# Four feature tiles at once, a normalised pair per quarter step, an earlier second attention and eight first products

## The chip, the cores and the metric

The kernel runs on one core of one Trainium2 chip. The metric is the device time of one launch in microseconds (us); the kernel before is given as the median of 3 runs.

## The reference

Two chained networks of two layers each work on x of 256 tokens by 1024 features, in fp32. Cut to what matters here:

```python
# first block, each of 2 layers
u = rms_norm(h, norm_mix[layer])
z, xbc, dt_raw, q, k, v, g_ssd, g_attn = split(u @ w_in[layer])
y_ssd = ssd_mixer(z, xbc, dt_raw, ...)          # convolution, state space, gated norm
y_attn = dilated_attention_mixer(q, k, v, ...)  # 8 kv heads, 3 windows each
merged = sigmoid(g_ssd) * (y_ssd @ w_ssd_branch) + sigmoid(g_attn) * (y_attn @ w_attn_branch)
h = h + merged @ w_out[layer]
u = rms_norm(h, norm_ffn[layer])
gate, up = split(u @ w_gate_up[layer])
h = h + (silu(gate) * up) @ w_down[layer]
# second block, each of 2 layers
proj = rms_norm_2(x, norm_g[i]) @ w_in[i]       # retention heads and block-sparse attention heads
x = x + concat(r_out, m_out) @ w_out[i]
gate = sigmoid(rms_norm_2(x) @ w_ple_gate[i])
e = rms_norm_2(p[i] @ w_ple[i], ple_norm_g[i])
x = x + gate * e
```

## The kernel before

**Products.** All activations lie with features on the 128 partitions. Every fp32 product is three: weight and activation are each split into a rounded high part and a low remainder, and high·high, high·low and low·high are summed in PSUM. TensorE (PE) is the engine that nearly all of this runs on. The weights come in one stream, planned ahead: the DMA queue of SP brings 1 MB pieces (`raw`, 3 buffers), each holding two units of 1024 columns; for each unit ScalarE (ACT) casts the high part (`wh`, L154) and VectorE (DVE) subtracts it (`wl`, L157). Where `pool_every` is 4, in the state-space part of the first block, GpSimd (POOL) subtracts every fourth unit. Each of `wh` and `wl` has 3 buffers, and a split is called two units ahead (`LEAD`).

**Shapes of products.** `outT` (L411) makes eight output tiles of 128 features in the order of `blocks` (L47): for the three matrices of 1024 by 1024 that end in the residual or in the gate (`w_out`, `w_out_2`, `w_ple_gate_2`), three feature tiles run together over all eight input tiles (72 matmuls), then the other five one after the other. Each of the first four tiles has a PSUM buffer of its own in pool `mm`, which has 3 buffers; they are handed to `evac` by twos, when both are complete. Later tiles share a buffer by twos. `pairA` makes two feature tiles (L449 to L451); `slab` makes two token tiles of 512 columns, four units long (L394 to L396). PSUM has two more pools, `tr` (2 buffers, transposes) and `ch` (3, small products).

**Background steps.** Generators lie in queues `bg`; the products call `tick`, which moves each queue on by one `yield`. `Norm.part` squares finished feature pairs and writes `uh`, `ul`. `Norm.steps` sums over features with products of ones (L232), takes the power on POOL (`rsqrt`, L363, L369), spreads the factor over partitions (L223), and then either copies it (`rb`, L256: the gate of the second block) or, where `vpair` holds, makes all eight normalised tiles (`nv`, L262) and their splits (`uh` L376 on ACT, `ul` L387 on DVE). `norm_ple` (L1018) does the like for `e`, with the product L1042 behind the power `gr`.

**Places that the change touches.** At the start, products of ones (L324) run while the first weights come. In `block1` (L703) the heads of attention A run behind the projections of the second half; attention B begins at the last pair of the B projections (f == 6), after A's steps have been run out, with one `yield` more per head (`late`). Behind `w_out`, two slabs of `w_gate_up` (p = 0, 1) run on the unnormalised tiles, each followed by a tanh on ACT (L825) and two DVE products (L826, L827) that read its PSUM buffers. In `block2` (L1052) the gate's `evac` (L1102) first runs the norm's steps out and then, tile by tile, does L1110 (DVE, reads PSUM), tanh (L1111), L1112 and L1113.

**Order.** Only SP's issues at the start are in a written order; elsewhere a scheduler places instructions by its own reckoning of times, so that a change of the program's order or of a wait can move instructions far from it.

Of the kernel before, what the change touches and what calls it, by code (L numbers as in the profile page):

```python
# [10 lines left out]
F32 = mybir.dt.float32  # L11
# [3 lines left out]
ALU = mybir.AluOpType  # L15
# [3 lines left out]
P = 128  # L19
# [16 lines left out]
LEAD = 2  # L36
WARM = 2
START1 = 2
# [8 lines left out]
def blocks(name):  # L47

    kt = {"w_ple_2": 2, "w_down": 22}.get(name)
    if kt:  # L50
        return [(k, f) for f in range(8) for k in range(kt)]
    pairs = (4, 6, 0, 2) if name == "w_out_2" else (0, 2, 4, 6)
    out = [(k + i, f) for k in pairs for f in range(3) for i in range(2)]
    return out + [(k + i, f) for f in range(3, 8) for k in pairs for i in range(2)]

# [116 lines left out]
class Norm:  # L172
# [73 lines left out]
    def steps(self, wait=1):  # L246
        net, nc = self.net, self.net.nc
        for _ in range(wait):
            yield
        self.factor()  # L250
        for _ in range(wait):
            yield
        rb = self.broadcast(self.r)
        if not self.vpair:
            self.rb = net.sp.tile([P, S], F32, tag="cb", name="rb")
            nc.scalar.copy(self.rb, rb)  # L256
            return
        self.vh, self.vl = net.pair([P, KD, S], "uh", "ul")
        for f in range(0, 8, 2):
            v = net.sp.tile([P, 2, S], F32, tag="qk", name="nv", bufs=QK_BUFS)  # L260
            for i in range(2):
                nc.vector.scalar_tensor_tensor(v[:, i, :], self.h[:, f + i, :], self.gain[:, f + i:f + i + 1], rb,  # L262
                                               ALU.mult, ALU.mult)
            net.split(self.vh[:, f:f + 2, :], self.vl[:, f:f + 2, :], v)
        if self.first:
            for _ in range(8):
                yield
            rb = self.broadcast(self.r1)
            for f in range(8):
                h = self.h[:, f, :]  # L270
                nc.vector.scalar_tensor_tensor(h, h, self.first[0][:, f:f + 1], rb, ALU.mult, ALU.mult)
                if f % 2:
                    yield
# [7 lines left out]
class Net:  # L281
# [129 lines left out]
    def outT(self, name, layer, get, evac, ticks=1):  # L411
# [7 lines left out]
        for n, (k, f) in enumerate(seq):  # L419
# [3 lines left out]
            if b not in bank:  # L423
                bank[b] = self.mm.tile([P, 2, S], F32, tag="mm", name="mm")
            ps = bank[b][:, f - b, :]
# [6 lines left out]
            if (n + 1) % (8 // ticks) == 0:  # L432
                self.tick()
            f &= ~1
            if left[f] == 0 and left[f + 1] == 0:
                if f < single:
                    evac(f, [(i, 1, bank.pop(i)[:, 0:1, :]) for i in (f, f + 1)])
                else:
                    evac(f, [(f, 2, bank.pop(f))])

# [54 lines left out]

    def attention(self, v, kT, q0, q1, q2, oh, ol, late=0):
        nc = self.nc
# [3 lines left out]
        for h in range(4):  # L501
# [26 lines left out]
            yield  # L528
            for _ in range(late):
                yield  # L530
            pt = self.transpose4([e[:, 0, 256:384], e[:, 0, 0:128], e[:, 0, 128:256]])
# [171 lines left out]
    def block1(self, l, h, n1):  # L703
# [32 lines left out]
        for f in range(0, 8, 2):  # L736
            ps = self.pairA("w_in", l, C_B + 128 * f, D, getu)
            self.conv_pair(l, ps, 16 + f, bc[:, f:f + 2, :])
            if f == 6:
                self.drain(qa)  # L740
                os.append(self.pair([P, 4, S], "A0", "A1"))
                qa.append(self.attention(*B, *os[1], 1))
        def halves(tiles):
# [110 lines left out]
    def add_half(self, h, norm):  # L854
        def evac(f, parts):
            for i, n, ps in parts:
                hf = h[:, i:i + n, :]
                self.nc.vector.scalar_tensor_tensor(hf, ps, 0.5, hf, ALU.mult, ALU.add)
            norm.part(f)
        return evac  # L860
# [144 lines left out]
    def ple(self, l):  # L1005

        ph, pl = self.pair([P, 2, S], f"A{2 * l}", f"A{2 * l + 1}")
        self.split(ph, pl, self.pT[l])
        e = [self.sp.tile([P, 4, S], F32, tag=f"B{2 * l + t}", name="e") for t in range(2)]
        self.e0.append(e)  # L1010

        def evac(f, parts):
            ps = parts[0][2]
            (self.nc.scalar.copy if f % 4 else self.nc.vector.tensor_copy)(e[f // 4][:, f % 4:f % 4 + 2, :], ps)

        self.outT("w_ple_2", l, lambda k: (ph, pl, k), evac)

    def norm_ple(self, l):  # L1018
# [17 lines left out]
        self.rsqrt(r, pss, 1.0 / D, EPS2)  # L1036
        yield
        yield
        yield
        prb = self.ch.tile([P, S], F32, tag="ch", name="ch")  # L1040
# [11 lines left out]
    def block2(self, l, x, n1):  # L1052
# [48 lines left out]

        def evac(f0, parts):  # L1102
            self.drain(*self.bg)
            if last and f0 == 6:
                parts = [(6 + i, 1, parts[0][2][:, i:i + 1, :]) for i in range(2)]
            for f, n, ps in parts:
                tg = sp.tile([P, 2, S], F32, tag="qk", name="tg", bufs=QK_BUFS)
# [6 lines left out]
                if last:  # L1114
                    nc.sync.dma_start(a["out"][128 * f:128 * (f + n), :].rearrange("(f p) t -> p f t", p=P), xf)
            if after:
                after.part(f0)

# [129 lines left out]
```

## Time and profile before

| | |
|---|---|
| median of 3 runs | 1598.61 us (1598.45 to 1598.75) |
| the profiled execution: time, span | 1603.87 us, 1602.1 us |
| mean granted TensorE clock | 0.985 |
| PE busy | 1549.7 us (97%) |
| DVE, ACT, POOL busy | 1166.4, 824.5, 466.5 us |

The span is from the first to the last instruction of the profiled execution; its time is 1.8 us more. PE's busy share says little on a stream of dependent products; what matters is where PE has nothing to do and what ends that, and where its clock is granted at half. Views used: PE's waits, the timeline by engine around the longest idle stretches, and the busy time with the granted clock in chosen stretches.

### The profile page before, as it was taken

To read this page: it belongs to the slowest core of one execution; us is meant where nothing else is said; L and a number is where in the kernel's file an instruction comes from. 1 tells how busy PE (TensorE), PEld (TensorE's weight loads), DVE (VectorE), ACT (ScalarE), POOL (GpSimd) and SP (SyncE) were. 2 spreads that over 40 slices of the span, in tenths; PEclk is the share of its full clock that TensorE was granted. 3 is DMA by queue.
4 is the path that set the end of the run, shared out by engine and by line. 5 is a ranking of instruction groups with operands and counts; after the bars stand their busy time and mean duration, and the time that the engine had idled before them with its cause. 6 is when DMAs were issued, how large, how long until landed. Compare 5 with 4: busy or idle time off the path is not lost. (4 is left out here: it accounts for less than half of the span.)

```text
span 1602.1 us, 28965 instructions
## 1 busy us (share of the span) xinstructions
PE 1549.7 (97%) x11900; PEld 1474.5 (92%) x11900; DVE 1166.4 (73%) x1760; ACT 824.5 (51%) x1268; POOL 466.5 (29%) x283
## 2 busy tenths in 40 slices
PE   7999999989989999999999899998999999999998
PEld 6899989989979999899998899997999979898987
DVE  6788988875576655668898786576565677777775
ACT  6444566654445444544466664454444554455443
POOL 3566355753010000076437566010000111211120
PEclk9999999999999999999999999999999999999999
DMA  8554453545545555654444445564555545444542
GB/s 295 175 181 177 161 183 132 186 156 192 181 158 184 184 185 184 210 188 155 159 159 162 154 158 202 190 210 167 185 187 188 179 157 184 155 161 164 185 152 80
DMA packets 42660, 280.65 MB, mean 175 GB/s; under 512 B 4864, under 2 KB 7040, under 8 KB 10016
## 3 DMA queue, kind: packets, MB, share of 16 engines
q1 hardware_dynamic: 40592, 267.20, 48.2%
q0 software_dynamic: 1936, 11.60, 1.9%
q8 instruction: 93, 1.52, 0.4%
q14 instruction: 39, 0.32, 0.1%
HBM read 274.53 MB, written 4.26 MB: 174 GB/s over the span
## 5 line engine op out<-in xcount | busy, mean ns | idle before, releaser
L157 DVE TENSOR_TENSOR wl<-raw,wh 128x1024 fp32r<-128x1024 f32 x456 | 602.3, 1322 | 300.9 <-ACT wh L154 298.1
L154 ACT CAST wh<-raw 128x1024 fp32r<-128x1024 f32 x488 | 510.9, 1048 | 574.1 <-PE mm L450 340.5
L451 PE MATMUL mm<-uh,wl 128*128 128x256 f32 x2112 | 592.7, 281 | 6.9 <-POOL wl L157 4.2
L449 PE MATMUL mm<-uh,wh 128*128 128x256 f32 x2112 | 596.6, 283 | 1.8 <-ACT wh L154 1.6
L450 PE MATMUL mm<-ul,wh 128*128 128x256 f32 x2112 | 590.3, 280 | 0.0
L451 PEld LDWEIGHTS mm<-uh,wl 128*128 128x128 f32 x2112 | 399.4, 189 | 9.1 <-POOL wl L157 4.9
L449 PEld LDWEIGHTS mm<-uh,wh 128*128 128x128 f32 x2112 | 398.6, 189 | 6.2 <-issue 3.3
L450 PEld LDWEIGHTS mm<-ul,wh 128*128 128x128 f32 x2112 | 399.7, 189 | 0.7 <-issue 0.5
L206 POOL TENSOR_TENSOR nsq<-nsq 128x512 f32<-128x512 f32 x18 | 30.1, 1675 | 479.7 <-ACT nsq L200 398.8
L157 POOL TENSOR_TENSOR wl<-raw,wh 128x1024 fp32r<-128x1024 f32 x32 | 80.1, 2504 | 65.4 <-ACT wh L154 62.7
L429 PE MATMUL mm<-A,wh 128*128 128x256 f32 x288 | 82.9, 288 | 4.7 <-ACT wh L154 4.0
L395 PE MATMUL mm<-wl,nu 128*128 128x512 f32 x192 | 80.1, 418 | 4.1 <-DVE wl L157 4.1
L394 PE MATMUL mm<-wh,nu 128*128 128x512 f32 x192 | 75.2, 414 | 8.9 <-DVE tg L827 8.9
L431 PE MATMUL mm<-A,wl 128*128 128x256 f32 x288 | 82.1, 286 | 0.0
L654 POOL TENSOR_TENSOR M<-M,cb 128x768 f32<-128x768 f32 x32 | 68.7, 2162 | 37.8 <-DVE cb L628 19.4
L396 PE MATMUL mm<-wh,nu 128*128 128x512 f32 x192 | 79.3, 414 | 0.0
L614 DVE SCALAR_TENSOR_TENSOR acc<-mm,feat,acc 128x255 f32<-128x255 f32 (+2 forms) x144 | 67.7, 475 | 6.6 <-ACT acc L612 5.3
L469 POOL TENSOR_TENSOR qT<-qT,rot 64x512 f32<-64x512 f32 x32 | 56.2, 1755 | 51.8 <-ACT qT L465 51.8
L470 POOL TENSOR_TENSOR qT<-qT,rp 64x512 f32<-64x512 f32 x32 | 62.3, 1947 | 28.3 <-DVE rp L467 28.2
L430 PE MATMUL mm<-A,wh 128*128 128x256 f32 x224 | 64.2, 286 | 0.0
L429 PEld LDWEIGHTS mm<-A,wh 128*128 128x128 f32 x288 | 55.5, 193 | 5.8 <-ACT wh L154 4.3
L431 PEld LDWEIGHTS mm<-A,wl 128*128 128x128 f32 x288 | 55.2, 192 | 0.3 <-DVE wl L157 0.3
(307 smaller groups left out, 3108.4 us busy)
## 6 DMA issues: line engine op xcount, KB each, us to landing
raw<-in_w_dram SPq DMA_DIRECT2D x243, 1024.0 KB, 4.8
abc<-scr POOLq DMA_DIRECT2D x8, 1024.0 KB, 5.6
es<-e POOLq DMA_DIRECT2D x4, 512.0 KB, 4.0
e<-es SPq DMA_DIRECT2D x4, 512.0 KB, 4.4
raw<-in_w_dram SPq DMA_DIRECT2D x2, 512.0 KB, 4.7
h<-in_xT_dram SPq DMA_DIRECT2D x2, 512.0 KB, 8.9
h<-in_xT_dram SPq DMA_DIRECT2D x1, 1024.0 KB, 4.8
hs<-h POOLq DMA_DIRECT2D x1, 1024.0 KB, 6.0
```

The source lines that it names most:

```text
L154: self.nc.scalar.copy(h, raw)
L157: eng.tensor_tensor(lo, raw, h.bitcast(F32), ALU.subtract)
L394: nc.tensor.matmul(ps, xh[:, k0 + k, ts], hw[:, k, :], start=start and k == 0, stop=False)
L395: nc.tensor.matmul(ps, xh[:, k0 + k, ts], lw[:, k, :], start=False, stop=False)
L396: nc.tensor.matmul(ps, xl[:, k0 + k, ts], hw[:, k, :], start=False, stop=stop and k == 1)
L429: nc.tensor.matmul(ps, hw[:, n % 8, :], xh[:, kx, :], start=opens, stop=False)
L431: nc.tensor.matmul(ps, lw[:, n % 8, :], xh[:, kx, :], start=False, stop=left[f] == 0)
L449: nc.tensor.matmul(ps, hw[:, k, :], xh[:, kx, :], start=j == 0 and k == 0, stop=False)
L450: nc.tensor.matmul(ps, hw[:, k, :], xl[:, kx, :], start=False, stop=False)
L451: nc.tensor.matmul(ps, lw[:, k, :], xh[:, kx, :], start=False, stop=j == n - 1 and k == 7)
L614: nc.vector.scalar_tensor_tensor(acc[:, j, k:S], ps[:, j, 0:S - k], w[:, 3 - k:4 - k], acc[:, j, k:S], ALU.mult, ALU.add)
L654: nc.gpsimd.tensor_tensor(m, m, cb[:, None, :].to_broadcast([P, 2, 384]), ALU.mult)
```

## The change

There are six edits. `WARM` goes from 2 to 8. `blocks` opens four feature tiles together, not three. In `outT` the fourth of them takes its buffer from pool `ch`, and each of the four is handed to `evac` by itself as soon as it is complete; `add_half`, `ple` and the gate's `evac` take the new arguments. `Norm.steps` yields after each of the first three normalised pairs. Attention B begins at f == 0 of the B projections, and `late` is gone. `norm_ple` waits five steps, not three, between the power and its broadcast.

```diff
-WARM = 2
+WARM = 8
...
-    out = [(k + i, f) for k in pairs for f in range(3) for i in range(2)]
-    return out + [(k + i, f) for f in range(3, 8) for k in pairs for i in range(2)]
+    out = [(k + i, f) for k in pairs for f in range(4) for i in range(2)]
+    return out + [(k + i, f) for f in range(4, 8) for k in pairs for i in range(2)]
...
             net.split(self.vh[:, f:f + 2, :], self.vl[:, f:f + 2, :], v)
+            if f < 6:
+                yield
...
-                bank[b] = self.mm.tile([P, 2, S], F32, tag="mm", name="mm")
+                pool, tag = (self.ch, "ch") if f == 3 and single else (self.mm, "mm")
+                bank[b] = pool.tile([P, 2, S], F32, tag=tag, name="mm")
...
-            f &= ~1
-            if left[f] == 0 and left[f + 1] == 0:
-                if f < single:
-                    evac(f, [(i, 1, bank.pop(i)[:, 0:1, :]) for i in (f, f + 1)])
-                else:
-                    evac(f, [(f, 2, bank.pop(f))])
+            if left[f] == 0 and (b == f < single or f > b):
+                evac(b, f + 1 - b, bank.pop(b)[:, 0:f + 1 - b, :])
...
-            for _ in range(late):
-                yield
...
-            if f == 6:
+            if f == 0:
                 self.drain(qa)
                 os.append(self.pair([P, 4, S], "A0", "A1"))
-                qa.append(self.attention(*B, *os[1], 1))
+                qa.append(self.attention(*B, *os[1]))
...
-        yield
-        yield
-        yield
+        for _ in range(5):
+            yield
```

Lines of the changed kernel are a few higher or lower in number; L262 is the same in both, and L387, L826, L827, L508, L510, L525, L614, L429 to L431 are now L389, L824, L825, L508, L510, L525, L612, L433 to L435.

DVE, at the slabs of `w_gate_up` in the first layer (`nv` and `ul` are the normalised tiles and their low parts, `tg` the gated product that frees a slab's PSUM buffer). Before:

```order
L157 TENSOR_TENSOR wl<-raw,wh 128x1024
L262 SCALAR_TENSOR_TENSOR nv<-h_4917,gains,ch 128x256 x8
L387 TENSOR_TENSOR ul<-nv,uh 128x512 x4
L826 SCALAR_TENSOR_TENSOR tg<-tg,mm 128x256 x2
L827 SCALAR_TENSOR_TENSOR tg<-tg,nrr,mm 128x256 x2
L157 TENSOR_TENSOR wl<-raw,wh 128x1024 x3
```

Now:

```order
L157 TENSOR_TENSOR wl<-raw,wh 128x1024
L262 SCALAR_TENSOR_TENSOR nv<-h_4923,gains,ch 128x256 x4
L824 SCALAR_TENSOR_TENSOR tg<-tg,mm 128x256 x2
L389 TENSOR_TENSOR ul<-nv,uh 128x512
L825 SCALAR_TENSOR_TENSOR tg<-tg,nrr,mm 128x256 x2
L389 TENSOR_TENSOR ul<-nv,uh 128x512
L262 SCALAR_TENSOR_TENSOR nv<-h_4923,gains,ch 128x256 x4
```

The two gated products stand behind four normalised tiles and one low part, not behind eight and four; the second layer has the same change, and on ACT the two tanh stand ahead of the casts `uh`.

PE, at the gate of the last layer (L223 spreads the factor; `mm_17008` and `mm_17021` are the last of the feature tiles that run together, `mm_17105` and `mm_17152` the tile that needs a buffer back). Before:

```order
L430 MATMUL mm_17008<-nu_16712,wh_16990 128x256
L431 MATMUL mm_17008<-nu_16710,wl_16991 128x256
L223 MATMUL ch_17072<-c0_80,nr_17040 128x128 x2
L429 MATMUL mm_17105<-nu_16709,wh_17021 128x256
L430 MATMUL mm_17105<-nu_16711,wh_17021 128x256
```

Now:

```order
L433 MATMUL mm_17021<-nu_16716,wh_17028 128x256
L434 MATMUL mm_17021<-nu_16718,wh_17028 128x256
L223 MATMUL ch_17079<-c0_80,nr_17047 128x128 x2
L435 MATMUL mm_17021<-nu_16716,wl_17029 128x256
L433 MATMUL mm_17021<-nu_16716,wh_17028 128x256
L434 MATMUL mm_17021<-nu_16718,wh_17028 128x256
L435 MATMUL mm_17021<-nu_16716,wl_17029 128x256
L433 MATMUL mm_17152<-nu_16715,wh_17063 128x256
```

L223 stood at the end of the 72 matmuls of three tiles, right before the matmul that needs a buffer back; it now stands after 92 of the 96 matmuls of four tiles. L232 stands after 55 of the gate's matmuls in both. The first gate of `block2` reads alike.

DVE, in the state-space part of the first layer (`m_1879` and `m_1854` belong to the last head of attention A, `m_2132` and `m_1924` to the first head of B; L614, now L612, is a step of the convolution). Before:

```order
L522 RECIPROCAL mx<-mx 128x2
L614 SCALAR_TENSOR_TENSOR acc<-mm,feat,acc 128x253
L157 TENSOR_TENSOR wl<-raw,wh 128x1024
L614 SCALAR_TENSOR_TENSOR acc<-mm,feat,acc 128x255
L617 SCALAR_TENSOR_TENSOR bc<-bc,acc 128x512
L525 TENSOR_SCALAR E<-E,mx 128x256
L526 TENSOR_SCALAR E<-E,mx 128x128
L614 SCALAR_TENSOR_TENSOR acc<-mm,feat,acc 128x254
L508 ISA E,m_2132<-ch,mask_a 128x256
```

Now:

```order
L612 SCALAR_TENSOR_TENSOR acc<-mm,feat,acc 128x253
L514 TENSOR_REDUCE mx<-m_1854 128x2
L508 ISA E,m_1924<-ch,mask_a 128x256
L508 ISA m_1924 128x1
L510 ISA E,m_1924<-ch,mask_a 128x128
L510 ISA m_1924 128x1
L516 TENSOR_SCALAR mx<-mx 128x2
L612 SCALAR_TENSOR_TENSOR acc<-mm,feat,acc 128x255
```

The first scores of B stood fifteen rows behind the last scores of A and now stand one row behind them; by the rows of before's durations up to two heads of attention stand ahead of weight splits that stood ahead of them (units 53 to 82 of the stream), and from unit 86 on DVE has done the same work by the same split as before.

## Rows read from the trace of the kernel before

**Rows 1.** PE's waits: line, released by: us in total, times, longest us.

```profile
PE mm L394 <- DVE tg L827: 8.9, 2, 4.5
...
PE mm L429 <- DVE tg L1110: 4.3, 2, 2.1
...
PE ch L1042 <- POOL gr L369: 2.1, 1, 2.1
```

**Rows 2.** Timeline of PE, first gate_up slabs: start, us, instruction, [idle before <-releaser].

```profile
478.17 0.77 PE L394 MATMUL mm<-wh,nu 128*128 128x512 f32 x1 [4.45 <-DVE tg L827]
```

**Rows 3.** Timeline of DVE, same stretch.

```profile
471.35 3.21 DVE L262 SCALAR_TENSOR_TENSOR nv<-h,gains,ch 128x256 f32<-128x256 f32 x8
474.48 2.49 DVE L387 TENSOR_TENSOR ul<-nv,uh 128x512 fp32r<-128x512 f32 x4
476.89 0.74 DVE L826 SCALAR_TENSOR_TENSOR tg<-tg,mm 128x256 f32<-128x256 f32 x2
477.55 0.86 DVE L827 SCALAR_TENSOR_TENSOR tg<-tg,nrr,mm 128x256 f32<-128x256 f32 x2
```

**Rows 4.** Timeline of ACT, same stretch.

```profile
472.25 0.62 ACT L376 CAST uh<-nv 128x512 fp32r<-128x512 f32 x1 [2.08 <-DVE nv L262]
...
475.20 1.08 ACT L825 ACTIVATE tg<-mm,nrh 128x256 f32<-128x256 f32 x2
```

**Rows 5.** Busy time by stretch, with granted clock (PEclk).

```profile
475.90:482.90 7.00, 4.73 (x11) 3.79 (x12) 3.23 (x7) 1.42 (x2) 0.00 (x0) 0.51 0.00 0
...
1582.00:1585.40 3.40, 3.40 (x18) 3.40 (x17) 1.46 (x5) 0.72 (x1) 0.00 (x0) 0.50 0.34 116
```

**Rows 6.** Timeline of PE, gate of the last layer.

```profile
1577.66 0.71 PE L223 MATMUL ch<-c,nr 128*128 128x128 f32 x4
1580.51 0.36 PE L429 MATMUL mm<-nu,wh 128*128 128x256 f32 x1 [2.14 <-DVE tg L1110]
```

**Rows 7.** Timeline of ACT, same gate.

```profile
1577.72 1.05 ACT L154 CAST wh<-raw 128x1024 fp32r<-128x1024 f32 x1 [2.23 <-PE mm L430]
1578.67 0.36 ACT L256 COPY rb<-ch 128x256 f32<-128x256 f32 x1
```

**Rows 8.** Timeline of DVE, same gate.

```profile
1578.80 1.23 DVE L157 TENSOR_TENSOR wl<-raw,wh 128x1024 fp32r<-128x1024 f32 x1 [1.98 <-ACT wh L154]
1579.94 1.08 DVE L1110 TENSOR_TENSOR tg<-mm,rb 128x256 f32<-128x256 f32 x3
```

**Rows 9.** Busy time by stretch, two state-space parts: PE, PEld, DVE, ACT, POOL, PEclk.

```profile
160.00:200.00 40.00, 40.00 (x333) 39.22 (x332) 37.04 (x96) 23.32 (x40) 14.57 (x10) 1.00 0.45 160
...
780.00:840.00 60.00, 58.62 (x480) 56.73 (x479) 57.45 (x132) 36.20 (x64) 16.27 (x11) 1.00 0.45 159
840.00:920.00 80.00, 74.68 (x614) 69.23 (x612) 64.92 (x105) 50.28 (x105) 49.14 (x28) 1.00 0.44 159
```

**Rows 10.** Line L508 by form: count, ns min/median/max; a head has three of each.

```profile
L508 DVE CUSTOM_DVE_ANT_0 E<-ch,mask_a x48: 402/416/426, 96.2 to 890.3; 128x256 f32<-128x256 f32 x48
```

**Rows 11.** Line L525 by form, columns as before.

```profile
L525 DVE TENSOR_SCALAR E<-E,mx x16: 336/1100/2542, 113.4 to 896.0; 128x256 f32<-128x256 f32 x16
```

**Rows 12.** Timeline of PE at the start.

```profile
0.98 1.22 PE L324 MATMUL ch<-ones 128*128 128x128 f32 x4 [0.98 <-POOL nhalf L320]
6.16 0.58 PE L429 MATMUL mm<-A,wh 128*128 128x256 f32 x1 [3.96 <-ACT wh L154]
...
6.76 0.41 PE L429 MATMUL mm<-A,wh 128*128 128x256 f32 x1
6.97 0.41 PE L430 MATMUL mm<-A,wh 128*128 128x256 f32 x1
...
11.85 0.28 PE L429 MATMUL mm<-A,wh 128*128 128x256 f32 x1
11.97 0.28 PE L430 MATMUL mm<-A,wh 128*128 128x256 f32 x1
...
22.37 0.50 PE L395 MATMUL mm<-wl,nu 128*128 128x512 f32 x1 [0.72 <-DVE wl L157]
```

More of the change, by code (lines that the diff above doesn't have):

```diff
@@ L494, in qkv_half, with attention @@
         return out
-    def attention(self, v, kT, q0, q1, q2, oh, ol, late=0):
+    def attention(self, v, kT, q0, q1, q2, oh, ol):
         nc = self.nc
@@ L854, in add_half, with evac @@
     def add_half(self, h, norm):
[L855 to L859, printed above, removed]
+        def evac(f, n, ps):
+            hf = h[:, f:f + n, :]
+            self.nc.vector.scalar_tensor_tensor(hf, ps, 0.5, hf, ALU.mult, ALU.add)
+            if n == 2 or f % 2:
+                norm.part(f & ~1)
         return evac
@@ L1010, in ple, with evac @@
         self.e0.append(e)
-        def evac(f, parts):
-            ps = parts[0][2]
+        def evac(f, n, ps):
             (self.nc.scalar.copy if f % 4 else self.nc.vector.tensor_copy)(e[f // 4][:, f % 4:f % 4 + 2, :], ps)
@@ L1100, in block2, with evac @@
         after = None if last else Norm(self, x, self.gains[:, G_2 + l + 1, :], EPS2, ("xs", "xs", "u", "u"))
-        def evac(f0, parts):
+        def evac(f0, n0, ps0):
             self.drain(*self.bg)
-            if last and f0 == 6:
-                parts = [(6 + i, 1, parts[0][2][:, i:i + 1, :]) for i in range(2)]
-            for f, n, ps in parts:
+            step = 1 if last and f0 == 6 else n0
+            for f, n, ps in [(f0 + i, step, ps0[:, i:i + step, :]) for i in range(0, n0, step)]:
                 tg = sp.tile([P, 2, S], F32, tag="qk", name="tg", bufs=QK_BUFS)
@@ L1115, in evac @@
                     nc.sync.dma_start(a["out"][128 * f:128 * (f + n), :].rearrange("(f p) t -> p f t", p=P), xf)
-            if after:
-                after.part(f0)
+            if after and (n0 == 2 or f0 % 2):
+                after.part(f0 & ~1)
         self.outT("w_ple_gate_2", l, n2.get, evac, 2)
```

## The prediction

> **What bounds the kernel now.** PE carries nearly everything, so I read first who PE waited for [rows 1], then the timelines around the longest waits, engine by engine, and last the granted clock behind them. Four waits stand out, two of a kind. Twice, at the gate_up slabs, PE waits for L827 on DVE, 8.9 us together; twice, at the gates of the second block, for L1110, 4.3 us together [rows 1].
>
> *gate_up.* PE stands still for 4.45 us and goes on at 478.17 [rows 2]. It needs a PSUM buffer back, which the first L827 frees. DVE is never idle meanwhile: it makes eight normalised tiles (3.21 us), four low parts (2.49 us), two L826 and only then L827 [rows 3]. None of the tiles is needed yet. ACT too runs its casts `uh` before the tanh at 475.20 [rows 4]. So the wait is one of order, not of work.
>
> *Gate.* L223 stands at 1577.66, right ahead of the matmul that needs a buffer back; PE goes on at 1580.51 [rows 6]. In between come a cast on ACT that started 0.06 us after L223 and keeps the copy `rb` until 1578.67 [rows 7], a split of 1.23 us on DVE, and L1110 [rows 8].
>
> *The clock.* Behind such waits the granted clock is half (1.2 instead of 2.4 GHz) for a while: 0.51 over 475.90 to 482.90, 0.50 over 1582.00 to 1585.40 [rows 5]. At half clock a stretch full of matmuls does half its work, so the second of these costs 3.4 / 2 = 1.7 us, and the first, of which PE used 4.73 us, some 2.35 us. Each long wait therefore has two prices, the idle time and what follows.
>
> The sum is made against the profiled execution of 1603.87 us, with its span of 1602.1 us and 1.8 us around it. That is 5.3 us above the median of the runs, 1598.61 us; I carry the difference over to the median. About 0.2%, 3.2 us, is what a measurement can tell from no change.
>
> **Part 1: four tiles at the gate.** Counted in matmuls, L232 stands where it stood, and L223 20 matmuls later. A matmul takes 0.12 us start to start (11.85 to 11.97 [rows 12]). Call T the start of L223 before. Before, PE resumed at T + 2.85 us (1577.66 to 1580.51 [rows 6]) with 120 matmuls left: T + 2.85 + 14.4 = T + 17.25. Now L223 starts at T + 2.4; by then the cast and split that stood in the way are done, because the buffer that they waited for came free at T in either case. What follows is L223 (0.71), the copy (0.36 [rows 7]), one L1110 (1.08 for three, so 0.36 [rows 8]) and some 0.25 us of hand-overs: resumed at T + 2.4 + 1.7, with 96 matmuls left, which is T + 4.1 + 11.5 = T + 15.6. Saved: 1.65 us. Four matmuls run under the chain, so the idle time left is about 0.6 us in place of 2.14. I expect no half clock behind so short a wait, which gives back 1.7 us more [rows 5]. That is 3.3 us a gate, 6.6 us for two; at least 2 times 1.65 = 3.3, if the clock falls all the same. What would be late next is nothing on PE: the next two weight units are split by then. The end after the last matmul is untouched. The buffer from `ch` costs nothing where three are there and the small products of the norm take one or two at a time; if L232 or L223 had to wait for it, a place could lose as much as the present wait, 2.14 us [rows 6], for which the order gives no sign. At `w_out` and `w_out_2` the same four tiles run together, but PE's waits name no buffer of theirs, so I count 0 there.
>
> **Part 2: quarter steps at gate_up.** By the order DVE now does four tiles (3.21 / 2 = 1.6 us, from 471.35 to about 472.95), two L826, one low part, L827. The tanh come first on ACT; their PSUM tiles are complete about six matmuls of a slab before PE stops, near 472.3, so both end near 473.4 (1.08 us for two [rows 4]). L826 then ends near 473.8. The low part must wait for its cast (0.62 us [rows 4], from 473.4 to 474.0) and ends near 474.65 (2.49 / 4 = 0.62 [rows 3]); the first L827, 0.43 us, near 475.1; PE goes on near 475.3 instead of 478.17. Saved: 2.85 us, with 1.6 us of the wait left. The rest, four tiles, two low parts and splits, is work under the second slab, which is some eleven us long. Bounds: 2.0 us if the casts or tanh come later than I reckon, 3.3 us if the scheduler's order leaves no hole. Both layers: 5.7 us. The half clock behind the wait (2.35 us in the first layer, less in the second) may stay, be halved or go: 0 to 4, and I take 1.0.
>
> **Part 3: attention B earlier.** One head costs DVE three L508 (0.416 us each [rows 10]) with their smaller companions and two scalings, of which L525 alone has a median of 1.10 us [rows 11]; by these rows about 4 us, an estimate. Up to two heads, some 8 to 9 us, come to stand ahead of splits. In the first layer DVE has 40.00 - 37.04 = 2.96 us of idle time in 160 to 200 us [rows 9], where this falls, and in the second 60.00 - 57.45 = 2.55 us over 60 us. What does not fit delays splits, which run up to two units ahead of PE. Against that, PE loses 80.00 - 74.68 = 5.3 us in 840 to 920 us, where DVE has 15 us to spare: work done earlier frees just this place. So from -8 (waits and half clock at 840 to 926 go) to +8; nearest is a small gain, and I take -1. Nothing else waits behind the attention's steps on SP; POOL gets the same additions earlier.
>
> **Part 4: eight products of ones.** They run from 0.98 us; four records take 1.22 us [rows 12], so 16 end near 4.8 us, before the first weights at 6.16. They cost nothing: PE idles there for 3.96 us. They may let the clock rise sooner. The first matmuls are 0.21 us apart (6.76 to 6.97 [rows 12]) and are 0.12 apart only from 11.85 on, behind 5.7 us of matmuls. (11.85 - 6.16) / 0.21 = 27 matmuls at 0.09 us less are 2.4 us; but PE then runs ahead into splits that are not ready, as at 22.37, where it waits for DVE anyway [rows 12]. I take 0.5, between 0 and 2.4. The Trainium skill ("TensorE: Matmul & The Clock Gate", Part 1: The HAM clock gate) says that the default is the throttled clock and that activity releases it; by that rule alone the sum would have the whole 2.4 us here, and no run so far shows whether products of ones do it.
>
> **Part 5: norm_ple.** Two yields more put L1042 later behind its power. The one wait there is 2.1 us [rows 1]; the order puts the first of the two products earlier among the slabs' matmuls, not later, so I count 0, between -5 (wait and the half clock behind it go) and +1.
>
> **Sum:** 6.6 + 5.7 + 1.0 + 1.0 + 0.5 = 14.8 us. I round down to 13.6, since each hand-over is taken at its best: 1598.6 - 13.6 = 1585.0 us, or 1590.3 us in a profiled execution.
>
> **Rivals.**
> *The clock stays low (1590 us).* The waits shrink, but half clock still follows each: 3.3 + 5.7 = 9.0 us. For it: 1.6 us of idle time are left at gate_up. Against it: the 0.6 us at the gates.
>
> *Everything goes (1576 us).* Half clock vanishes at gate_up (3 us more) and the stops at 840 to 926 us go (6 us more). For it: DVE's spare time there; against it: the scheduler moves some hundreds of instructions, and some new stop is likely.
>
> *The attention eats it (1597 us).* Splits come 6 us late in each layer, 9 us of work less 3 of idle time: 13.6 - 12 = 1.6 us gained.
>
> *Slower: DVE and POOL get in each other's way (1606 us).* The place is the state-space part, 160 to 200 and 780 to 840 us. L525, one shape, takes from 336 to 2542 ns [rows 11]; a stretch where DVE's work and POOL's additions fall together can make DVE's work longer. At 6 us late, 3 us for four operations stretched by 0.75 each, and 1.7 us of half clock, a layer loses 10.7 us, both 21.4: 1598.6 - 13.6 + 21.4 = 1606. It decides from 8.4 us a layer on. Against it: PE lost nothing in 160 to 200 us with DVE at 37.04 of 40 us [rows 9]. The Trainium skill ("GPSIMD Engine Reference", 1. Specifications) says that POOL shares its SBUF interfaces with VectorE and that they contend when DVE has two SBUF inputs or a two-port mode; the spread of L525 agrees, and the time by that rule is this rival's.
>
> *The change does not do what it says.* L223 or the tiles could stand elsewhere than meant; the order shows them moved, so this is left at the cases above.
>
> **How the numbers follow.** Forecast 0.52 (1579 to 1588), clock stays low 0.22, everything goes 0.10, attention eats it 0.08, slower 0.08. The first three are faster by over 3.2 us: 0.84. Same: 0.08. Slower: 0.08. The range leaves out the slower case, half of the case at 1597 and half of the best: 1577 to 1597 us.
>
> **What would show it.** Right: PE's waits for L825 (old L827) near 1.6 us each and for L1105 (old L1110) below 0.8; no half clock behind the gates; PE full in 160 to 200 us. Wrong: the gate's wait still over 1.5 us with a cast between L223 and the copy; DVE full and PE waiting for `wl` around 160 to 200 or 780 to 840 us; a new half-clock stretch in the state-space part; L232 or L223 waiting for a `ch` buffer.

## The result: 1580.8 us, and the profile after

| | median | runs | ratio to before, 95% interval |
|---|---|---|---|
| before | 1598.53 us | 4 | |
| changed | 1580.79 us (1579.01 to 1581.76) | 4 | 0.9888, 0.987 to 0.9905 |
| changed, again beside the experiments | 1582.60 us | 6 | 0.9919, 0.9896 to 0.9943 |
| changed, a third time | 1579.76 us | 6 | 0.9888, 0.9869 to 0.9907 |

The change makes the kernel 17.7 us faster (16.3 by the mean of the three ratios). 1585.0 was forecast, with 1577 to 1597 as the range. The sum came out nearly right, in part by luck: of its terms two did, and the rest was made up of one gain that was mis-sized, one loss that was not seen and one term with the wrong sign in one layer. One run further down, of six products of ones, took 1879 us at a mean granted clock of 0.753; it is left out of its version's ratio, and as it was the profiled one, that version's profile is not read.

The page of the changed kernel, span and first line of busy time:

```profile
span 1577.2 us, 28986 instructions
...
PE 1540.3 (98%) x11912; PEld 1467.8 (93%) x11912; DVE 1160.2 (74%) x1760; ACT 822.9 (52%) x1268; POOL 463.6 (29%) x283
```

PE's waits in the changed kernel (line, released by: us in total, times, longest us), to be laid beside [rows 1]:

```profile
PE mm L451 <- DVE wl L157: 8.5, 5, 2.4
PE tr L385 <- DVE E L526: 4.6, 5, 1.9
...
PE mm L433 <- ACT O L378: 2.7, 2, 1.3
PE mm L396 <- DVE tg L825: 2.2, 2, 1.1
...
PE mm L434 <- DVE O L389: 1.9, 2, 0.9
...
PE mm L433 <- DVE tg L1105: 0.9, 2, 0.4
```

The 8.9 us at gate_up are 2.2, the 4.3 us at the gates 0.9, and the 2.1 us for `gr` are gone. But other lines have grown. The transposes of attention now wait 4.6 us for `E` (0.7 before), and behind the gated heads `O` costs 2.7 and 1.9 us (1.5 and 1.1 before). The waits of the first block for `wl` have moved rather than grown: 8.5 us for DVE's splits now; before, 5.1 us for DVE's and 4.2 us for POOL's.

**gate_up.** DVE and then PE in the changed kernel, the stretch of [rows 2 to 4]:

```profile
468.70 0.75 DVE L824 SCALAR_TENSOR_TENSOR tg<-tg,mm 128x256 f32<-128x256 f32 x2
469.37 0.69 DVE L389 TENSOR_TENSOR ul<-nv,uh 128x512 fp32r<-128x512 f32 x1
469.97 0.87 DVE L825 SCALAR_TENSOR_TENSOR tg<-tg,nrr,mm 128x256 f32<-128x256 f32 x2
470.75 0.69 DVE L389 TENSOR_TENSOR ul<-nv,uh 128x512 fp32r<-128x512 f32 x1
471.35 1.26 DVE L262 SCALAR_TENSOR_TENSOR nv<-h,gains,ch 128x256 f32<-128x256 f32 x3
```

```profile
470.59 0.47 PE L396 MATMUL mm<-wh,nu 128*128 128x512 f32 x1 [1.08 <-DVE tg L825]
```

Only one low part stands before L825, and the tanh are done by the time DVE reaches L824, so nothing waits for ACT. 1.08 us of idle time are left of 4.45, and half clock follows it in none of the three profiled executions of the changed kernel.

**Gate of the last layer.** PE, ACT, DVE in the changed kernel, against [rows 6 to 8]:

```profile
1558.31 0.60 PE L223 MATMUL ch<-c,nr 128*128 128x128 f32 x4
...
1559.11 0.28 PE L435 MATMUL mm<-nu,wl 128*128 128x256 f32 x1
1559.84 0.39 PE L433 MATMUL mm<-nu,wh 128*128 128x256 f32 x1 [0.44 <-DVE tg L1105]
```

```profile
1558.95 0.37 ACT L256 COPY rb<-ch 128x256 f32<-128x256 f32 x1 [1.88 <-PE ch L223]
```

```profile
1559.36 1.42 DVE L1105 TENSOR_TENSOR tg<-mm,rb 128x256 f32<-128x256 f32 x4 [1.03 <-ACT rb L256]
```

The copy now waits for L223 itself, no longer for a cast; 0.44 us are left of 2.14.

**The gated heads.** PE at the product behind them, in the changed kernel:

```profile
1367.43 1.04 PE L385 MATMUL tr<-c,b 128*128 128x128 f32 x8
1369.80 0.74 PE L433 MATMUL mm<-O,wh 128*128 128x256 f32 x4 [1.33 <-ACT O L378]
1371.48 0.39 PE L434 MATMUL mm<-O,wh 128*128 128x256 f32 x1 [0.94 <-DVE O L389]
```

ACT there, in the changed kernel:

```profile
1366.78 1.99 ACT L154 CAST wh<-raw 128x1024 fp32r<-128x1024 f32 x2 [3.38 <-PE mm L434]
1368.68 1.06 ACT L378 CAST O<-tr 128x512 fp32r<-128x512 f32 x2
```

and in the kernel before:

```profile
1387.25 1.05 ACT L154 CAST wh<-raw 128x1024 fp32r<-128x1024 f32 x1 [2.29 <-PE mm L430]
1388.53 1.07 ACT L376 CAST O<-tr 128x512 fp32r<-128x512 f32 x2 [0.23 <-PE tr L383]
```

With four tiles the transposes of the second half of the heads stand behind 48 matmuls, two whole weight units, instead of 36. Two casts of weights (and two splits on DVE) stand ahead of the casts `O` that PE waits for, where one stood. Behind both places the granted clock is half (busy time by stretch, PEclk in the third column from the right):

```profile
1372.00:1375.40 3.40, 3.40 (x18) 3.40 (x18) 0.00 (x0) 0.00 (x0) 0.00 (x0) 0.50 0.35 149
1529.00:1532.40 3.40, 3.40 (x18) 3.40 (x17) 0.00 (x0) 0.00 (x0) 0.00 (x0) 0.50 0.41 173
```

### The profile page after: what moved, and what is told of

Its sections match the earlier page's. It is cut to its first block, busy times and chain, and to the rows that moved or that the text cites. A ratio compares the mean times of both kernels' runs of the same rounds, so it can differ in the third digit from the quotient of the medians.

```text
span 1577.2 us, 28986 instructions
## 1 busy us (share of the span) xinstructions
PE 1540.3 (98%) x11912; PEld 1467.8 (93%) x11912; DVE 1160.2 (74%) x1760; ACT 822.9 (52%) x1268; POOL 463.6 (29%) x283
## 4 chain that ended last, share of the span: by engine, by line
PE 85%; DVE 9%; ACT 2%; issue 2%; POOL 1%; DMA 0%; DVEq 0%; SPq 0%; POOLq 0%; ACTq 0%
PE mm L449 17%; PE mm L451 16%; PE mm L450 16%; PE mm L434 6%; PE mm L435 6%; PE mm L433 6%; PE mm L397 4%; PE mm L396 4%; PE mm L398 4%; DVE wl L157 3%; PE ch L662 2%; PE tr L385 1%; ACT wh L154 1%; DVE acc L612 1%; DVE E L525 1%
## 5 line engine op out<-in xcount | busy, mean ns | idle before, releaser
L157 DVE TENSOR_TENSOR wl<-raw,wh 128x1024 fp32r<-128x1024 f32 x456 | 603.8, 1327 | 273.4 <-ACT wh L154 270.6
L157 POOL TENSOR_TENSOR wl<-raw,wh 128x1024 fp32r<-128x1024 f32 x32 | 79.1, 2471 | 67.6 <-ACT wh L154 62.5
L433 PE MATMUL mm<-A,wh 128*128 128x256 f32 x288 | 81.5, 285 | 1.4 <-ACT wh L154 1.4
L435 PE MATMUL mm<-A,wl 128*128 128x256 f32 x288 | 81.3, 285 | 0.1
L397 PE MATMUL mm<-wl,nu 128*128 128x512 f32 x192 | 76.5, 400 | 2.7 <-DVE wl L157 2.6
L652 POOL TENSOR_TENSOR M<-M,cb 128x768 f32<-128x768 f32 x32 | 70.0, 2204 | 25.7 <-ACT M L651 17.7
L398 PE MATMUL mm<-wh,nu 128*128 128x512 f32 x192 | 75.3, 395 | 0.0
L396 PE MATMUL mm<-wh,nu 128*128 128x512 f32 x192 | 72.1, 398 | 3.0 <-DVE tg L825 2.2
L612 DVE SCALAR_TENSOR_TENSOR acc<-mm,feat,acc 128x255 f32<-128x255 f32 (+1 forms) x144 | 67.2, 475 | 4.3 <-ACT acc L610 2.9
L433 PEld LDWEIGHTS mm<-A,wh 128*128 128x128 f32 x288 | 55.1, 191 | 1.9 <-ACT wh L154 1.7
L435 PEld LDWEIGHTS mm<-A,wl 128*128 128x128 f32 x288 | 54.6, 191 | 0.6 <-DVE wl L157 0.6
```

The costliest lines, as they stand in the source:

```text
L157: eng.tensor_tensor(lo, raw, h.bitcast(F32), ALU.subtract)
L396: nc.tensor.matmul(ps, xh[:, k0 + k, ts], hw[:, k, :], start=start and k == 0, stop=False)
L397: nc.tensor.matmul(ps, xh[:, k0 + k, ts], lw[:, k, :], start=False, stop=False)
L398: nc.tensor.matmul(ps, xl[:, k0 + k, ts], hw[:, k, :], start=False, stop=stop and k == 1)
L433: nc.tensor.matmul(ps, hw[:, n % 8, :], xh[:, kx, :], start=opens, stop=False)
L435: nc.tensor.matmul(ps, lw[:, n % 8, :], xh[:, kx, :], start=False, stop=left[f] == 0)
```

## A second profile of the kernel before, and a ledger by stages

The profiled execution of before was one of the slowest of its kernel, and the two profiles above differ by 24.9 us where the medians differ by 17.7. So the kernel before was profiled again.

> The kernel before as it is, for a second profile: its one profiled execution took 1603.9 us, 5.3 us above the median of its runs. Theory A, that profile had one rare disturbance: the power on POOL that took 5.17 us at 44 us, with 2.11 us of waiting and 6.8 us of half clock behind it, will be as short as elsewhere (0.7 to 1.7 us). Theory B, the power is slow at this place every time, and the 5 us are half clock that follows the same waits in some executions and not in others: the waits agree within 0.1 us, the stretches of half clock do not.

Measured: 1596.85 us median of 8 runs, ratio 1.0003 (0.9985 to 1.0021). Cores view of the first profile and of the second:

```profile
core 0: 1602.1 us, clock 0.985
```

```profile
core 0: 1593.0 us, clock 0.993
```

Theory B holds. PE waits 4.44 us twice at gate_up, 2.14 twice at the gates and 2.11 for `gr`, as in the first profile, and the slow power is there again:

```profile
44.09 5.17 POOL L369 TENSOR_TENSOR gr<-rs_v,nhalf 128x2 f32<-128x2 f32 x1 [2.98 <-DVE rs_v L368]
```

DVE while that power runs:

```profile
43.93 1.89 DVE L387 TENSOR_TENSOR ul<-nv,uh 128x512 fp32r<-128x512 f32 x3
45.73 1.22 DVE L157 TENSOR_TENSOR wl<-raw,wh 128x1024 fp32r<-128x1024 f32 x1
46.87 0.69 DVE L387 TENSOR_TENSOR ul<-nv,uh 128x512 fp32r<-128x512 f32 x1
47.47 1.22 DVE L157 TENSOR_TENSOR wl<-raw,wh 128x1024 fp32r<-128x1024 f32 x1
```

What differs is the half clock: up to the last matmuls, nine stretches of 44 us together in the first, five of 20 us in the second. In the second, none follows the gates (busy time by stretch):

```profile
1572.60:1580.00 7.40, 7.34 (x61) 7.37 (x62) 5.27 (x13) 3.44 (x6) 0.00 (x0) 1.00 0.20 68
1414.70:1422.00 7.30, 7.29 (x60) 7.30 (x61) 6.36 (x16) 5.48 (x11) 0.00 (x0) 1.00 0.42 146
```

So the same wait is followed by half clock in one execution and not in another. Half of 44 and of 20 us are 12 us apart, enough for the 9.1 us between the two executions. That the spread of the kernel's other runs (1589 to 1602 us beside the experiments) comes from the same is likely but not shown, as they have no profile. One execution's stretch is a chance, then, not a price.

For the stages I therefore use when the k-th cast `wh` starts, counted from the first, in each trace, minus the same in the second profile of before. The table gives the change over each stage in us; "changed" has three executions, "undone" the runs below.

| stage (units of the weight stream) | first profile of before | changed, three executions | undone or altered part |
|---|---|---|---|
| start and first slabs (0 to 40) | +3.2 | -5.1, -5.0, -2.7 | 2 products of ones: +1.3; 5 products: +2.8 |
| first layer's state-space part (40 to 105) | +0.9 | +5.0, +5.6, +5.2 | attention B late: +0.3, +0.6, -0.4 |
| ... to the end of gate_up (105 to 200) | 0.0 | -5.9, -5.8, -9.4 | no quarter steps: -4.5, -0.6 |
| second layer's state-space part (200 to 310) | +2.4 | -3.8, -5.3, -3.8 | attention B late: -1.0, -1.1 |
| second gate_up (310 to 380) | 0.0 | -4.7, -5.0, -4.6 | no quarter steps: +0.5, -2.5 |
| second block (380 to 488) | +2.6 | -1.3, -0.1, -1.2 | three tiles: +3.1; three at w_out_2 alone: -7.2 |
| whole span | +9.1 | -15.8, -15.5, -16.3 | |

Each stage carries its half clock with it, so single cells move by 2 to 4 us; the sign of each line is the same in all executions of the changed kernel, though -0.1 in the last stage is nothing. In the first layer's state-space part, PE's waits come to 9.2 us in the changed kernel's first profile and 6.8 in the second profile of before, and 10.2 us against 3.4 run at half clock: 2.4 us more of waiting and 3.4 of work lost, more than enough for the +5.0.

## The experiments

**Two products of ones.**

```diff
-WARM = 8
+WARM = 2
```

> The changed kernel with two products of ones instead of eight at the start, all else as changed. The changed kernel took 1580.8 us in four runs. Theory A, the start is worth several us: in the two profiles the changed kernel is 3.3 us ahead after the tenth weight unit and 8.9 us after the fifteenth, so without the eight products it should be 3 to 9 us slower, 1584 to 1590 us, with the half-clock stretches at 32 and 49 us back. Theory B, PE at the start only runs ahead into splits that are not ready, and the 8.9 us are mostly a slow power on POOL in the one profile of before: 0 to 1 us slower, 1581 to 1582 us.

Measured: 1583.86 us (6 runs), ratio 0.9921 (0.9902 to 0.9941), some 3 us slower than the changed kernel by the medians and 7.6 us by the spans of the two profiles (1584.8 against 1577.2). PE waits again as before (timeline of PE):

```profile
30.69 0.57 PE L397 MATMUL mm<-wl,nu 128*128 128x512 f32 x1 [1.47 <-DVE wl L157]
...
49.47 0.71 PE L1038 MATMUL ch<-c,gr 128*128 128x128 f32 x4 [1.88 <-POOL gr L371]
```

In the changed kernel no wait of PE is left between 25 and 50 us, and its powers of `gr` take (timeline of POOL):

```profile
41.48 1.16 POOL L371 TENSOR_TENSOR gr<-rs_v,nhalf 128x2 f32<-128x2 f32 x1
...
50.14 3.18 POOL L371 TENSOR_TENSOR gr<-rs_v,nhalf 128x2 f32<-128x2 f32 x1
```

Theory A in kind. But it doesn't say what the products do: keep PE busy, or move other instructions. The instruction order tells that two to five products give one order of the work at the start, six to twelve the other; by the traces of five and eight it differs on DVE up to 140 us, not only in the first 60. So five and six were run side by side with the changed kernel.

> The changed kernel once more, as it is, on the chip on which the next three run, so that they can be compared with it. Expected 1579 to 1582 us, as in its first four runs, and PE's waits at the same places: 1.08 us twice at the gate_up slabs, 0.44 us twice at the gates, 1.33 and 0.94 us behind the gated heads. What half clock follows may differ from execution to execution.

> The changed kernel with five products of ones instead of eight. By the instruction order, two to five products give one order of the work up to about 60 us (the order of the kernel before there), six to twelve give the other (the changed kernel's). Theory A, the gain at the start is that of the order: five products take as long as two, 3 us more than eight, with PE's waits of some 1.5 us at 29 us and 1.9 us at 48 us. Theory B, the gain is that of PE being busy before the first weights, and so of the clock: most of it comes with five, 0 to 1 us more than eight.

> The changed kernel with six products of ones instead of eight: the instruction order is that of eight, but PE idles 0.5 us longer before the first weights. Theory A, order alone: the same time as eight within 0.5 us, without the waits at 29 and 48 us. Theory B, the clock: slower than eight by part of the 3 us, in step with the number of products.

| products | order | median | ratio, 95% interval |
|---|---|---|---|
| 5 | of two | 1586.44 us | 0.9947, 0.9926 to 0.9969 |
| 6 | of eight | 1580.07 us | 0.9895, 0.987 to 0.992 |
| 8 | of eight | 1582.60 us | 0.9919, 0.9896 to 0.9943 |

Between five and six products lie 0.5%, between six and eight nothing that can be measured, and PE's waits of 1.48 us (L397) and 1.88 us (L1038) are in five's profile as in two's. Theory A: the gain goes with the order, which changes between five and six products. That the scheduler changes it because it reckons the start as longer is my reading; that six products are free of those two waits is not shown by a profile.

**Three tiles at once.**

```diff
-... for f in range(4) ...   ... for f in range(4, 8) ...
+... for f in range(3) ...   ... for f in range(3, 8) ...
-pool, tag = (self.ch, "ch") if f == 3 and single else (self.mm, "mm")
+pool, tag = self.mm, "mm"
```

> The changed kernel with three feature tiles at once instead of four in the three 1024 by 1024 products into the residual and the gate (each still handed on by itself when complete). Theory A, the four tiles help at the gates and harm at the gated heads: at the gates PE waits 2.1 us again in place of 0.44 and half clock follows, 3.3 us each, 6.6 us in all; at the two products behind the gated heads PE waits 0.73 and 0.54 us in place of 1.33 and 0.94 us and the half clock behind them (3.4 us, worth 1.7) goes, 2.7 us each, 5.4 us in all: net 1.2 us slower, 1581 to 1583 us. Theory B, only the gates matter, as the prediction had it: 6.6 us slower, 1587 us.

Measured: 1581.64 us, ratio 0.9902 (0.9886 to 0.9918). PE's waits:

```profile
PE mm L433 <- DVE tg L1105: 4.3, 2, 2.1
...
PE mm L433 <- ACT O L378: 1.5, 2, 0.7
```

Theory A: the gates' waits are back at 2.1 us, the gated heads' are down, and the two nearly cancel in the time. In the profile half clock follows the gates (1398.9 and 1559.3 us) and not the gated heads, two stretches in place of two. The second block alone is 4.4 us longer there than in the changed kernel's first profile (3.2 and 4.3 against the other two). Of the 4.4, 2.3 us are more waiting of PE, and 1.7 us are one more stretch of half clock, at 1276.0, behind a wait for `wl` that the changed kernel has too: not the tiles' doing.

**No quarter steps.**

```diff
             net.split(self.vh[:, f:f + 2, :], self.vl[:, f:f + 2, :], v)
-            if f < 6:
-                yield
```

> The changed kernel without the steps between the normalised pairs: all four pairs are made at once. Theory A, the wait at the gate_up slabs comes back whole with the half clock behind it: 4.45 us in place of 1.08 in each layer, 6.7 us, and half clock behind them worth 2.35 and 1.5 us: 7 to 10.6 us slower, 1588 to 1591 us. Theory B, the idle time comes back but the clock does not fall or was falling already elsewhere: 6.7 us slower or less, 1585 to 1587.5 us.

Measured: 1582.70 us (1580.46 to 1589.77), ratio 0.9925 (0.9902 to 0.9948): too wide to size, so it was run again beside the changed kernel.

> The changed kernel as it is, again as the one to compare the next three with on their chip. Expected 1579 to 1585 us, the span of its runs so far.

> The changed kernel without the steps between the normalised pairs, once more, now beside the changed kernel on one chip: the first time it was measured beside others only, 1582.7 us with runs from 1580.5 to 1589.8, which leaves the size of the term open. Theory A, the wait of 4.45 in place of 1.08 us is on the path in both layers and half clock follows: 7 to 10 us slower than the changed kernel on this chip. Theory B, the idle time is partly given back further on, since splits and loads gain a lead in it: 2 to 4 us slower.

Measured: 1585.30 us, ratio 0.9928 (0.9906 to 0.995), against 1579.76 us and 0.9888 for the changed kernel: 5.5 us by the medians, 6.4 by the ratios. PE's waits have the old row back:

```profile
PE mm L394 <- DVE tg L823: 8.9, 2, 4.5
```

6.7 us of idle time came back, so it was on the path and little of it was regained further on. The time lies between the two theories: more than B's 2 to 4 us, less than A's 7 to 10. Half clock follows both waits in both profiles (3.4 us at 473, then 6.8 at 1080.5 and 1087.3), yet the times don't show all of A's price for it.

**Attention B late again.**

```diff
-            if f == 0:
+            if f == 6:
...
-                qa.append(self.attention(*B, *os[1]))
+                qa.append(self.attention(*B, *os[1], 1))
```

> The changed kernel with the second attention begun at the last pair of the B projections and its extra step per head back, as before the change. By the two profiles the first layer's state-space part lost 5.3 us with the change and the second layer's won about 6. Theory A, both come from the earlier attention: undone, the first layer wins 4 to 5 us, the second loses 5 to 6, and the time is 1580 to 1583 us, with the two halves visible in the profile. Theory B, the loss in the first layer comes from other instructions that the scheduler moved: then undoing it leaves that loss and takes the gain of the second layer, 1585 to 1587 us.

Measured: 1574.61 us (1571.17 to 1580.86), ratio 0.9867 (0.9847 to 0.9888): some 6 us faster than the changed kernel, more than theory A allowed. By the ledger the first layer wins 5 us and the second loses 3. Busy time over 160 to 200 us, of the changed kernel and of this one (PE, PEld, DVE, ACT, POOL):

```profile
160.00:200.00 40.00, 38.82 (x315) 37.66 (x315) 38.53 (x104) 24.27 (x41) 10.86 (x9) 1.00 0.49 163
```

```profile
160.00:200.00 40.00, 40.00 (x334) 39.17 (x333) 37.26 (x90) 25.17 (x42) 13.26 (x9) 1.00 0.53 186
```

PE was never idle there with attention B late; with B early it loses 1.2 us. The wait, in the changed kernel, on PE, then DVE, then POOL:

```profile
187.29 0.52 PE L385 MATMUL tr<-c,E 128*128 128x128 f32 x3 [1.18 <-DVE E L526]
```

```profile
179.13 0.34 DVE L525 TENSOR_SCALAR E<-E,mx 128x256 f32<-128x256 f32 x1
...
184.50 2.44 DVE L525 TENSOR_SCALAR E<-E,mx 128x256 f32<-128x256 f32 x1 [0.51 <-POOL E L524]
186.87 0.27 DVE L526 TENSOR_SCALAR E<-E,mx 128x128 f32<-128x128 f32 x1
```

```profile
184.43 2.37 POOL L157 TENSOR_TENSOR wl<-raw,wh 128x1024 fp32r<-128x1024 f32 x1
```

The same scaling takes 0.34 us at 179 and 2.44 at 184.50, where POOL's split starts 0.07 us before it and ends 0.14 us before it does. PE's transposes wait for it. The second place is larger, DVE then POOL then PE:

```profile
291.86 2.31 DVE L615 SCALAR_TENSOR_TENSOR xs<-xs,acc 128x512 f32<-128x512 f32 x1
294.10 3.37 DVE L157 TENSOR_TENSOR wl<-raw,wh 128x1024 fp32r<-128x1024 f32 x1
```

```profile
286.80 6.83 POOL L652 TENSOR_TENSOR M<-M,cb 128x768 f32<-128x768 f32 x3 [1.67 <-DVE cb L626]
293.59 2.80 POOL L157 TENSOR_TENSOR wl<-raw,wh 128x1024 fp32r<-128x1024 f32 x1
```

```profile
297.53 0.58 PE L451 MATMUL mm<-O,wl 128*128 128x256 f32 x1 [2.40 <-DVE wl L157]
```

A split that takes 1.23 us alone takes 3.37 beside POOL, and 6.8 us of half clock follow. With attention B late PE has one stop of 2.40 us of this kind in the first layer, not two. Such meetings are not new: the kernel before has five L525 of over 1.8 us among its sixteen, as the changed kernel has. Before, PE's transposes waited 0.7 us for `E`; now they wait 4.6.

**Late in the first layer, early in the second.**

```diff
-            if f == 0:
+            if f == (0 if l else 6):
...
-                qa.append(self.attention(*B, *os[1]))
+                qa.append(self.attention(*B, *os[1], 0 if l else 1))
```

> The changed kernel with the second attention begun late, as before the change, in the first layer and early, as changed, in the second. Late in both layers gave 1574.6 us against some 1581. Theory A, the early start costs in the first layer only, about 7 us by the profiles, and is worth 0 to 2 us in the second: 6 to 8 us faster than the changed kernel on this chip, about 1574 us. Theory B, it costs about the same in each layer: 3 us faster.

Measured: 1574.48 us, ratio 0.9851 (0.9827 to 0.9875), beside 1579.76 us and 0.9888 of the changed kernel: 5.3 us faster. The cost is in the first layer. Its ledger there is +0.6 (changed +5.0 to +5.6), and in the second layer -4.0, as in the changed kernel, where late has -1.0: early is worth some 3 us there by the profiles. Against late in both (1574.61 us, on another chip) the times don't tell.

**A version that beats both.** Attention B late in both layers, and three tiles at once at `w_out_2` alone:

```diff
-    out = [(k + i, f) for k in pairs for f in range(4) for i in range(2)]
+    n = 3 if name == "w_out_2" else 4
+    out = [(k + i, f) for k in pairs for f in range(n) for i in range(2)]
```

> A version meant to beat both: the changed kernel with the second attention begun at the last pair of the B projections as before the change (1574.6 us by itself), and with three feature tiles at once in the product behind the gated heads (w_out_2) while w_out and the gate keep four. Theory A, the waits behind the gated heads shrink from 1.33 and 0.94 us to 0.73 and 0.54 us and the half clock behind them goes: 2.7 us in each layer, 5.4 us: 1569 us. Theory B, the clock falls elsewhere instead: only the 2.0 us of idle time are won, 1572.5 us.

Measured: 1572.56 us (1567.69 to 1574.44), ratio 0.9851 (0.9826 to 0.9876), beside 1582.60 us and 0.9919 of the changed kernel: 10 us faster than it and 24 us faster than before. PE's wait behind the gated heads is shorter than either theory had it, 0.49 and 0.48 us, and no half clock follows it in the profile:

```profile
PE mm L434 <- ACT O L379: 1.0, 2, 0.5
```

The three tiles are 4.9 us of that by the ledger (-7.2 in the second block against -2.3 with attention late alone), 2.0 us by the medians, which are from different chips; so the time doesn't tell which of the two theories holds for the clock.

**Not run.** With three steps put back between power and broadcast in `norm_ple`, the instruction order of the changed kernel stays the same on every engine: that edit does nothing beside eight products. Beside two it does: there the order of 86 to 146 us changes with it. In that stretch the profiles of two and of five products have waits of PE for `E` of 1.70 us (at 118 or 119 us) and 0.7 us (at 138 or 139) that neither the kernel before nor the changed one has. So a part of what two and five products cost can be that edit's, and no run separates the two. Whether the `late` step alone, without the later start, would have kept the transposes from waiting was not tried.

## Why the prediction was right, and where its steps were not

By the ledger the four parts come to about +4, +7, -2 and +6 us, where 6.6, 6.7, 1.0 and 0.5 were forecast. Two errors of some 3 us each cancel one of 5 to 6, which is luck. Of the signs that were named, those for the waits at gate_up and the gates and for the clock behind the gates came true; but PE is not full in 160 to 200 us, and new stretches of half clock stand in the state-space parts (at 297 to 300 us in all three executions, near 839 in two), which was on the list for being wrong.

**Part 1, four tiles.** At the gates it was right: 0.6 us of idle time forecast, 0.44 found, L223 and the copy where the working had them. The 1.7 us of half clock a gate was taken in full; the second profile of before has none there, so its mean is lower. The sentence that failed is "PE's waits name no buffer of theirs, so I count 0 there". At `w_out_2` the buffer was not the point: more matmuls ahead of the transposes put another unit's cast and split between them and PE. That costs 1.0 us of idle time in each layer (1.33 + 0.94 against 0.73 and 0.54), and half clock followed in both layers in all three executions of the changed kernel. (In the six other profiles with four tiles there it follows in both layers three times, in one layer twice, in none once, so that price too is a chance.) So the edit is worth less than 6.6 us: 0.8 us by the medians of three tiles against four, 3 to 4 by the ledger.

**Part 2, quarter steps.** The mechanism was right, and the size: 5.7 us and 1.0 for the clock were forecast, 5.5 to 6.4 measured. The working had the tanh end 2 us after the normalised tiles begin; they ended before these begin, so the wait left is 1.08, not 1.6 us.

**Part 3, attention B earlier.** The step that failed is "nearest is a small gain, and I take -1". The ends, -8 to +8 us, hold what was found: about +5 us in the first layer and about -3 in the second by the ledger, +2 net; by the medians of the undone run it is +5 to +6 net, and that gap stays open. The working set DVE's idle time (2.96 us) against the extra work and let what did not fit delay splits. What showed in PE's waits was not the total but which instructions met, and where: DVE operations beside POOL's ran 2.7 to 7 times as long (3.37 against 1.23 us, 2.44 against 0.34), about as often as before, but now PE's transposes wait right behind them. That was the mechanism of the slower rival, at half its price, in one layer. Whether the earlier start or the lost `late` step puts the transposes there is not separated. In the second layer the waits at 840 to 926 us went as described, 5.7 us of them; three new ones, 1.20, 0.60 and 1.87 us, came at 812, 830 and 839 us, with half clock behind the last in two of three executions.

**Part 4, products of ones.** The term was mis-sized: 0.5 us, where the timed runs give 3 to 5 and the ledger 4 to 8, because it was costed as PE's clock. The products changed the scheduler's order of the start, and with it the waits for L157 at 29 us and for `gr` at 48 us went, with the half clock behind them. The changed order stood there to be read: L232 and the `norm_ple` products stand elsewhere among the slabs' matmuls. The wait for `gr` that Part 5 priced, with its half clock, at up to 5 us thus went, but by this order and not by Part 5's edit, which does nothing beside eight products.

**The Trainium skill's clock rule** ("TensorE: Matmul & The Clock Gate", Part 1: The HAM clock gate) was weighed as worth the whole 2.4 us. In three of the nine profiled executions with eight products the granted clock is full before 5.4 us and the first matmuls are 0.12 us apart, as that rule would have it. (In the others they are 0.21 us apart, as before; the spacing is the sign, since the view gives 1.00 also where no clock is on record yet.) Then it falls, as here in the version that beats both (busy time by stretch):

```profile
4.50:7.80 3.30, 1.35 (x9) 0.97 (x8) 1.63 (x2) 1.18 (x2) 0.00 (x0) 1.00 0.97 328
7.90:11.30 3.40, 3.40 (x18) 3.40 (x18) 2.60 (x4) 1.33 (x2) 0.00 (x0) 0.50 0.97 372
```

PE idled from 4.7 to 6.1 us in between. By the twentieth unit that execution is 3.5 us ahead of the second profile of before and the other two with the early clock 4.2 each; the changed kernel's three, without it, are 4.2, 4.0 and 3.0: the early clock bought nothing that shows.

**What stays open.** By the ratios the undone parts add up to some 6 us (products 3 to 5, steps 6, tiles 0 to 2, attention -4 to -6), where the whole change is 16 to 18. Each of them is uncertain by 3 us, and the spread of half clock enters each anew. By the ledger the parts come to about 15 (start 6, first layer -5, quarter steps 7, second layer 3, second block 4), which fits the whole (15.5 to 16.3). I take the ledger for where the time went, and the timed runs for which version is faster.

## What to carry to other kernels

Before costing an edit by what it adds, look in the instruction order for what else it moves: several us here came with eight small matmuls whose own work gains nothing that shows. A wait of PE for a buffer is often one of order, and splitting the work ahead of the release into steps takes it away. When an engine's work is moved earlier, ask which other engine's instructions it will then run beside, not only whether its idle time is large enough.

## What the runs showed that I had not expected

- A DVE operation on SBUF that begins while a POOL operation runs can last until that ends: L525 2.44 us beside a POOL split of 2.37 (0.34 alone), L157 3.37 us beside one of 2.80 (1.23 alone). In the traces of before and changed 22 of the 32 L525 begin under a POOL operation, and every one ends 0.15 to 0.16 us after it; the other ten take 0.34 to 0.35 us, also where POOL begins later. L614, which reads PSUM, is never held: 63 of before's begin under a POOL operation and none takes over 0.49 us. The Trainium skill ("GPSIMD Engine Reference", 1. Specifications) says that the two share their SBUF interfaces; the traces agree.
- Half clock follows a wait of the same place and length in some executions only: 2.14 us at the gates twice in one profile of before, never in the other.
- The power of 128 by 2 elements on POOL takes 5.17 us at one place in every execution with the first order (44.34, 44.09, 44.25, 43.99 us), 1.16 and 3.18 us in the other order, and 0.70 to 1.72 us elsewhere. What PE paid for it stands in [rows 1]. It is the same meeting the other way round: the power begins while DVE makes low parts and splits one right after the other, and ends 0.57 us after the last of them (48.69 and 49.26 us in the second profile of before; 52.75 and 53.33 for the 3.18 us). In the thirteen profiles read, the 60 powers `gr` that begin under a split, a low part or L617 take over 1 us, and the 70 others 0.70 to 0.72. So the place of DVE's splits also sets how long a power lasts; no run moved the splits alone.
